# A two-layer hybrid encoder on one core: the rotary chain spread over seven pieces of products, weight splits ranked behind and powers in front, memory's operands made on GpSimd

## The chip, the core and the metric

The kernel runs on one core of one Trainium2 chip. The time is that of one execution on the device in microseconds (us); several runs are made and their median is told. Five engines work side by side, each taking its own instructions strictly in the order in which the program lists them, and each waiting on the others through semaphores: TensorE (PE, matrix products; PEld is its loading of weights), VectorE (DVE), ScalarE (ACT), GpSimd (POOL) and SyncE (SP), which here issues the transfers (DMA).

## The reference

x is 512 tokens by 1024, float32, and passes through two layers. Each layer adds three things to x, each computed from an RMS-normalised copy:

```
x += W_out [ NA-heads(h) || GQA-heads(h) ]        h = RMSNorm(x), one projection w_in
x += MemoryCrossAttention(RMSNorm(x), RMSNorm(mem))   4 heads, 256 memory tokens
x += ConvFFN(RMSNorm(x))                          SwiGLU, width-3 convolution over positions
```

The first has eight heads of neighbourhood attention (NA: each token sees a window of an 8 x 64 grid) and eight query heads on two key-value heads of full attention (GQA). The GQA queries and keys are normalised per head over their 64 channels, multiplied by a gain, and turned by a rotary table:

```
g_q = apply_axial_rope(rms_norm(g_q, q_norm), cos, sin)      # q; k likewise with k_norm
out = stack([x1 * c - x2 * sn, x1 * sn + x2 * c])            # the rotation of a pair of channels
```

The memory's keys and values are `(RMSNorm(mem) * norm_mem_kv) @ w_mem_kv`, for each layer with its own gain.

## The kernel before

**Precision.** Products run in a short float format (fp32r) on split operands: every operand is written as `hi` (a cast) plus `lo` (what the cast lost), and each product is three: hi x hi, hi x lo, lo x hi. So each weight tile that comes from DRAM (`raw`) needs a cast on ACT (`hi`, L255) and a subtraction on POOL (`lo`, L256); this is a *weight split*, made by `emit_split`. Four pairs of hi/lo tiles rotate, so a cast can run only when the products of the weight tile four places earlier are done.

**Layout.** Tokens lie along the free axis (512 columns), channels along the 128 partitions. A projection of 128 output channels is 24 products of 512 columns: 8 slices of input channels by three. The kernel hands them out in *pieces*: generators (`project_qk`, `gqa_project`, `out_na`, ...) that yield after 12 products or so.

**Order.** The attention is a software pipeline (`weave`): at each step the scores of unit s, the normalising of unit s-1, the transposes of unit s-2 and so on are issued, and between them `Filler.run` puts pieces of projections on PE, as many as a budget in nanoseconds allows. PE and SP keep the order in which the Python code issues (`keep_in_program_order`). ACT, DVE and POOL do not: a list scheduler, with a timeline of its own, orders their instructions by a running number, the priority (`tc.cur_priority`, low first), among those which it believes ready. The result is a fixed order per engine; on the chip nothing overtakes.

**Late work.** `Late` holds functions until so many pieces later; `Filler.step` ticks it after each piece. The rotation of one GQA projection, `gqa_rope` (L785), works on a product tile `pm` through it:

- at once: `xs` = gain x pm (L790, ACT), `sq` = pm squared (L791, ACT), `cc` = gain x pm x cosine table (L792, DVE);
- `swap`, one piece later: four transfers swap channel halves of `xs` into `xr` on the SP queue; eight short products with `pairs` sum the squares per head (the *pairs product*, tile `tr`); two small DVE instructions (L801, L804);
- `rotate`, one piece later: on POOL the power -0.5 (L809), its broadcast into `sq` (L810), sine table times `xr` (L811), plus `cc` (L812);
- `norm`, two pieces later: eight short products with the identity turn the broadcast round into a tile `pr` (the *broadcast product*, tile `mm`), DVE multiplies it by `xr` (L819), and ACT and DVE split the result into hi and lo (L616/L620 for k, L634/L636 for q).

There are five such chains in a layer: k, then query pairs 0, 1, 2, 3 (`GQA_ORDER` has v between 1 and 2). PSUM has four accumulators for `mm`, two for `tr` and two for `sc`; a tile keeps its accumulator until the last reader has run.

**Memory.** `memory_prepare` (L488) makes the memory's operands, eight slices of channels by 256 tokens: ACT multiplies by the gain and casts (L502), DVE computes the rest (L503). It runs in the GQA stage by `MEM_STEPS`.

Of the kernel before, what the change touches and what calls it, by code (L numbers as in the profile page):

```python
# [1 line left out]

# [1 line left out]

# [8 lines left out]
AF = mybir.ActivationFunctionType  # L13
ALU = mybir.AluOpType
# [4 lines left out]
P = 128  # L19
# [5 lines left out]
NB = S // P  # L25
KC = D // P
HD = 64
# [21 lines left out]
GQA_FILL = [2300] * 16 + [3000] * 4  # L49
MEM_FILL = [1, 1, 1, 2, 1, 0, 0, 2, 0, 1, 2]  # L50
MEM_STEPS = [1, 0, 1, 1, 1, 1, 1, 1, 1] + [0] * 11
N_RAW, N_W, AHEAD, AHEAD_HELD, N_WARM, N_LATE, N_FIRST = 3, 4, 2, 5, 10, 4, 3


class InOrder:


    def __init__(self, tc, engine):
        self.tc, self.engine = tc, engine

    def __getattr__(self, name):
        op = getattr(self.engine, name)
        return lambda *a, **k: self.tc.keep_in_program_order(op(*a, **k))  # L63
# [12 lines left out]
        return self.tc.keep_in_program_order(self.engine.matmul(out, lhsT, rhs, **k))  # L76


class Switched:

    def __init__(self, tc, engine, ordered):
        self.tc, self.engine, self.ordered = tc, engine, ordered

    def __getattr__(self, name):
        op = getattr(self.engine, name)
        if self.ordered[0]:
            return lambda *a, **k: self.tc.keep_in_program_order(op(*a, **k))
        return op  # L90


class PartsView:
# [83 lines left out]
def encoder_kernel(ctx: ExitStack, tc: tile.TileContext, t: dict, out: bass.AP):  # L177
    nc = tc.nc
    PE, SP = Counted(tc, nc.tensor), InOrder(tc, nc.sync)
    late = Late()  # L180
    ACT_IN_ORDER = InOrder(tc, nc.scalar)
    ordered = [False]
    ACT, DVE, POOL = [Switched(tc, e, ordered) for e in (nc.scalar, nc.vector, nc.gpsimd)]

    cpool = ctx.enter_context(tc.tile_pool(name="cpool", bufs=1))
    xpool = ctx.enter_context(tc.tile_pool(name="xpool", bufs=1))
# [2 lines left out]
    tpool = ctx.enter_context(tc.tile_pool(name="tpool", bufs=10))  # L189
    spool = ctx.enter_context(tc.tile_pool(name="spool", bufs=24))  # L190
    psum = ctx.enter_context(tc.tile_pool(name="psum", bufs=2, space=PSUM))

    uid = [0]

    def nm(s):
        uid[0] += 1
        return f"{s}_{uid[0]}"

    def rtile(shape, dt=F32R):
        return rpool.tile([P, *shape], dt, tag="r", name=nm("r"), padded_shape=[P, *pad(shape)])  # L200
# [24 lines left out]
    f = lambda ap: ap.bitcast(F32)  # L225
# [3 lines left out]
    done = [0]  # L229
# [11 lines left out]
    def emit_split(act=ACT, cuts=2):  # L241
        n = len(ready)
        key, loads, nk, ncol, eng = plan[n]
        raw = raws[n]
        raws[n] = None
        if key[0] in ("up", "down", "memq", "memo"):
            cuts = 1
        if eng[1:] == "r":
            hi, lo = rtile((nk, ncol)), rtile((nk, ncol))
        else:  # L250
            hi = wpool.tile([P, nk, ncol], F32R, tag="hi", name=nm("hi"))
            lo = wpool.tile([P, nk, ncol], F32R, tag="lo", name=nm("lo"))
        for i in range(cuts):
            k = slice(nk * i // cuts, nk * (i + 1) // cuts)
            act.copy(hi[:, k], raw[:, k])  # L255
            (POOL if eng[0] == "P" else DVE).tensor_sub(lo[:, k], raw[:, k], f(hi)[:, k])  # L256
        ready.append((hi, lo))

    def get_w(key, ahead=AHEAD):
# [115 lines left out]
    mhalf = cpool.tile([P, 16], F32, name="mhalf")  # L375
    nc.vector.memset(mhalf, -0.5)

    def rsqrt(src, n, scale):

        v = small(n)  # L380
        DVE.tensor_scalar(v, src, scale, EPS, op0=ALU.mult, op1=ALU.add)
        r = small(n)
        POOL.tensor_tensor(r, v, mhalf[:, :n], op=ALU.pow)  # L383
        return r

    def row_rep(rstd, n, tag, bufs):
# [9 lines left out]
    class Norm:  # L396


        def __init__(self, gcol=None, l=None, cols=slice(0, S)):
            self.gcol, self.l, self.acc, self.last, self.cols, self.n = gcol, l, None, None, cols, cols.stop - cols.start  # L400
            if gcol is not None:
                self.hi, self.lo = [xpool.tile([P, KC, S], F32R, tag="xg", name=nm("xg"), bufs=2) for _ in range(2)]
                self.ops = [(self.hi[:, c, :], self.lo[:, c, :]) for c in range(KC)]
# [85 lines left out]
    def memory_prepare(l, raw=None):  # L489

        mops.clear()
        if raw is None:
            raw = load_mem()
            yield
            yield
        for c in range(KC):
            if c % 2 == 0:
                mg = rtile((2, 2, MEMN))
            g = par[:, l, G_MKV + c : G_MKV + c + 1]
            hi, lo = mg[:, 0, c % 2, :], mg[:, 1, c % 2, :]  # L500
            src = raw[c // 4][:, c % 4, :]
            ACT.activation(hi, src, AF.Copy, scale=g)  # L502
            DVE.scalar_tensor_tensor(lo, src, g, f(hi), op0=ALU.mult, op1=ALU.subtract)  # L503
            mops.append((hi, lo))
            if c % 2 == 1:
                yield
# [42 lines left out]
    for l in range(DEPTH):  # L549
# [63 lines left out]
        def split_k(pm, kt, near):  # L613
            rows = [(slice(64 * j, 64 * j + 64), slice(64 - 64 * j, 128 - 64 * j)) for j in range(2)]
            for k, (r, o) in zip(kt, rows):
                ACT.copy(k[r, 0], pm[r])  # L616
                if near:
                    ACT.copy(k[o, 0], pm[r])
            for k, (r, o) in zip(kt, rows):
                DVE.tensor_sub(k[r, 1], pm[r], f(k[r, 0]))  # L620
                if near:
                    DVE.tensor_sub(k[o, 1], pm[r], f(k[r, 0]))

            def double():
                for k, (r, o) in zip(kt, rows):
                    SP.dma_start(f(k[o]), f(k[r]))

            if not near:
                late(2, double)
# [156 lines left out]
        def gqa_rope(g, pm):  # L786

            gain = qkg[:, l, 0:1] if g != "k" else qkg[:, l, 1:2]
            xs, xr, sq, cc = tmp(), tmp(), tmp(), tmp()
            ACT.activation(xs, pm, AF.Copy, scale=gain)  # L790
            ACT.activation(sq, pm, AF.Square)  # L791
            DVE.scalar_tensor_tensor(cc, pm, gain, gtab[0][:, 0], op0=ALU.mult, op1=ALU.mult)  # L792

            def swap():
                for i in range(4):
                    SP.dma_start(xr[32 * i : 32 * i + 32], xs[32 * (i ^ 1) : 32 * (i ^ 1) + 32])
                pv = ps_t()
                for b in range(NB):
                    PE.matmul(pv[:, 2 * b : 2 * b + 2], sq[:, b * P : (b + 1) * P], pairs, start=True, stop=True)
                v = small(2 * NB)  # L800
                DVE.tensor_tensor(v.rearrange("p (b j) -> p b j", j=2), pv[:, 0 : 2 * NB].rearrange("p (b j) -> p b j", j=2),  # L801
                                  r2[0].unsqueeze(2).to_broadcast([P, NB, 2]), op=ALU.mult)

                DVE.tensor_scalar(v, v, *((1.0 / HD, EPS) if g == "k" else (1.0, EPS * HD)), op0=ALU.mult, op1=ALU.add)  # L804
                late(1, lambda: rotate(v))

            def rotate(v):
                r = small(2 * NB)
                POOL.tensor_tensor(r, v, mhalf[:, : 2 * NB], op=ALU.pow)  # L809
                POOL.tensor_copy(sq.rearrange("p (b d) -> p b d", d=HD), r.unsqueeze(2).to_broadcast([P, 2 * NB, HD]))  # L810
                POOL.tensor_mul(xr, xr, gtab[0][:, 1])  # L811
                POOL.tensor_add(xr, cc, xr)  # L812
                late(2, norm)

            def norm():
                pr = ps_mm()
                for b in range(NB):
                    PE.matmul(pr[:, b * P : (b + 1) * P], sq[:, b * P : (b + 1) * P], ident, start=True, stop=True)
                DVE.tensor_mul(pr, xr, pr)  # L819
                if g == "k":  # L820
                    gk.extend(rtile((2, S)) for _ in range(2))
                    split_k(pr, gk, False)
                else:
                    gq[g] = rtile((2, S))
                    split_q(pr, gq[g])

            late(1, swap)


        ga, gpt = {}, {}  # L830
# [134 lines left out]

        if l > 0:
            load_bias(0)
        ordered[0] = False
        units = [project_v(p) if n == "v" else project_qk(n, p) for n, p in NA_ORDER]
        nns = []  # L970
        attn_fill = Filler(
# [2 lines left out]
            close_rows("outg", 2, PartsView(parts, 4), lambda k: whole[k], lambda: nns.append(Norm(G_MQ, l)) or nns[0],  # L974
                       memory_values(1)))
        attn_fill.step(N_FIRST if l == 0 else N_FIRST + 5)
        ordered[0] = False

        def na_quanta(s):
            if s == 3:  # L980
# [97 lines left out]
        fill.finish()  # L1078


        ordered[0] = False
        ffn = nn
        acts = {}

# [220 lines left out]
```

## Time and profile before

| | us |
|---|---|
| median of 3 runs | 1454.72 (1453.51 to 1455.85) |
| the profiled execution | 1452.22 |
| its span, first to last instruction | 1450.4 |
| PE busy | 1377.7 (95%) |
| PEld busy | 1174.0 (81%) |
| DVE busy | 842.4 (58%) |
| ACT busy | 705.6 (49%) |
| POOL busy | 704.0 (49%) |
| mean granted TensorE clock | 0.978 of full |

How to read the views: *slices* are 40 equal parts of the span, a digit is a busy share in tenths, and PEclk is the TensorE clock that was granted, in tenths. *Waits* name who waited for whom, with the sum in us, the number of times and the longest. *Stretches* give, for a part of the span, busy us of PE, PEld, DVE, ACT and POOL, each with a count of instructions, then the granted clock, the share of the DMA engines and GB/s. *Groups* are instructions of one line and shape: count, busy us, mean ns of one, idle time before them and what ended it. The *timeline* has start, length, engine, line, and in brackets how long the engine idled before and what released it.

In the first layer the first softmax of the neighbourhood attention is at 50 us (L702), the first of the GQA stage at 175 us (L852), the first scores of the memory attention are reduced at 318 us (L1029), and the feed-forward part starts at 385 us (L1114). The five rotations stand between 107 us (the first L792) and 182 us, and in the second layer between 817 and 895 us (the last L819).

### The profile page before, as it was taken

What the parts mean: (1) busy time and instruction counts of PE and PEld (TensorE: products, weight loads), DVE (VectorE), ACT (ScalarE), POOL (GpSimd) and SP (SyncE); (2) the same over time, 40 slices, a digit from 0 to 9 for tenths busy, and PEclk for the clock granted to TensorE, in tenths of its full rate; (3) what the DMA queues carried; (4) which work ended last, traced back from release to release, by engine and by line L of the source; (5) the groups of instructions that cost most, each with busy time, mean ns of one, the idle gap of its engine ahead of it and who ended that gap; (6) DMA issues with size and microseconds to landing.
All of it is one profiled execution on the core that took longest, in us unless ns stands there. A gap on an engine that the chain in (4) does not pass through costs nothing. (4 is left out here: it accounts for less than half of the span.)

```text
span 1450.4 us, 19227 instructions
## 1 busy us (share of the span) xinstructions
PE 1377.7 (95%) x7092; PEld 1174.0 (81%) x7092; DVE 842.4 (58%) x1437; ACT 705.6 (49%) x1308; POOL 704.0 (49%) x509
## 2 busy tenths in 40 slices
PE   7999689999999999999999887999899999999997
PEld 6987579877888888888888766898788888888887
DVE  5664387446488258448446545764637861871874
ACT  5674377656444233333556644776554432431441
POOL 2356546653544444444645555566254444444451
PEclk8998899999999999999999988999999999999999
DMA  7552312321333333332355323124223333323321
GB/s 231 139 149 79 100 30 67 80 87 56 90 99 94 98 99 88 104 102 81 112 155 157 103 70 87 44 74 117 58 59 102 102 101 89 100 86 105 98 77 58
DMA packets 218173, 138.83 MB, mean 96 GB/s; under 512 B 5984, under 2 KB 211040, under 8 KB 218080
## 3 DMA queue, kind: packets, MB, share of 16 engines
q1 hardware_dynamic: 218080, 137.60, 33.2%
q8 instruction: 56, 0.92, 0.3%
q14 instruction: 37, 0.30, 0.1%
HBM read 125.00 MB, written 2.10 MB: 88 GB/s over the span
## 5 line engine op out<-in xcount | busy, mean ns | idle before, releaser
L256 POOL TENSOR_TENSOR lo<-raw,hi 128x1024 fp32r<-128x1024 f32 (+2 forms) x268 | 498.2, 1871 | 542.9 <-ACT hi L255 522.9
L76 PE MATMUL mm<-xg,hi 128*128 128x512 f32 x1984 | 627.5, 398 | 2.3 <-ACT xg L63 2.0
L76 PEld LDWEIGHTS mm<-xg,hi 128*128 128x128 f32 x1984 | 376.4, 192 | 79.2 <-ACT xg L63 2.4
L255 ACT CAST hi<-raw 128x512 fp32r<-128x512 f32 (+2 forms) x276 | 224.1, 836 | 350.6 <-PE mm L76 299.7
L76 PE MATMUL mm<-xg,lo 128*128 128x512 f32 x992 | 391.9, 395 | 0.0
L76 PE MATMUL mm<-r,hi 128*128 128x512 f32 (+1 forms) x1160 | 336.7, 374 | 2.7 <-DVE r L451 2.0
L76 PEld LDWEIGHTS mm<-r,hi 128*128 128x128 f32 x1160 | 211.1, 189 | 41.5 <-DVE r L451 2.8
L1129 DVE SCALAR_TENSOR_TENSOR t<-t,par,t 128x7 f32<-128x7 f32 (+1 forms) x352 | 203.8, 646 | 34.0 <-ACT t L1122 34.0
L76 PEld LDWEIGHTS mm<-xg,lo 128*128 128x128 f32 x992 | 189.9, 191 | 41.1 <-DVE lo L256 0.5
L76 PE MATMUL mm<-r,lo 128*128 128x512 f32 (+1 forms) x580 | 216.1, 373 | 0.0
L76 PEld LDWEIGHTS mm<-r,lo 128*128 128x128 f32 x580 | 109.5, 189 | 19.3
L457 POOL TENSOR_SCALAR t<-t,s 128x512 f32<-128x512 f32 (+1 forms) x112 | 66.0, 603 | 120.5 <-DVE s L852 62.5
L1114 DVE TENSOR_TENSOR t<-mm,rep 128x512 f32<-128x512 f32 x88 | 60.1, 687 | 77.6 <-PE mm L76 62.3
L1131 ACT ACTIVATE t<-t 128x512 f32<-128x512 f32 x44 | 27.9, 633 | 138.8 <-DVE t L1129 138.8
L1135 DVE TENSOR_TENSOR r<-t,r 128x512 fp32r<-128x512 f32 x44 | 90.5, 2056 | 7.3 <-ACT r L1134 4.1
L1158 DVE TENSOR_TENSOR xT<-xT,mm 128x512 f32<-128x512 f32 x32 | 21.9, 685 | 106.8 <-PE mm L76 106.8
L76 PE MATMUL sc<-r,r 128*128 128x256 f32 (+1 forms) x352 | 74.2, 343 | 4.3 <-DVE r L451 1.8
L63 PE MATMUL tr<-ident,t 128*128 128x128 f32 x456 | 63.1, 275 | 14.4 <-DVE r L451 8.5
L63 PEld LDWEIGHTS tr<-ident,t 128*128 128x128 f32 x456 | 52.8, 141 | 23.3 <-issue 12.6
L1122 ACT ACTIVATE t<-t,par 128x512 f32<-128x512 f32 x88 | 66.8, 806 | 2.4 <-DVE t L1114 2.4
L76 PE MATMUL mm<-r,r 128*128 128x256 f32 (+1 forms) x428 | 62.0, 297 | 0.0
L76 PEld LDWEIGHTS sc<-r,r 128*128 128x128 f32 x352 | 52.9, 195 | 11.2 <-ACT r L450 3.0
(133 smaller groups left out, 1534.3 us busy)
## 6 DMA issues: line engine op xcount, KB each, us to landing
raw<-in_w_up SPq DMA_DIRECT2D x88, 512.0 KB, 3.9
raw<-in_w_in SPq DMA_DIRECT2D x34, 512.0 KB, 5.0
raw<-in_w_down SPq DMA_DIRECT2D x32, 448.0 KB, 3.9
raw<-in_w_mem_kv SPq DMA_DIRECT2D x16, 512.0 KB, 3.8
raw<-in_w_down SPq DMA_DIRECT2D x16, 512.0 KB, 4.3
r<-in_bias SPq DMA_DIRECT2D x16, 384.0 KB, 5.7
r<-r SPq DMA_DIRECT2D x22, 256.0 KB, 5.1
raw<-in_w_out SPq DMA_DIRECT2D x8, 512.0 KB, 4.6
```

The source lines that it names most:

```text
L63: return lambda *a, **k: self.tc.keep_in_program_order(op(*a, **k))
L76: return self.tc.keep_in_program_order(self.engine.matmul(out, lhsT, rhs, **k))
L255: act.copy(hi[:, k], raw[:, k])
L256: (POOL if eng[0] == "P" else DVE).tensor_sub(lo[:, k], raw[:, k], f(hi)[:, k])
L457: eng.tensor_scalar(e, e, sums[:, col : col + 1], 1.0, op0=ALU.mult, op1=ALU.mult)
L1114: DVE.tensor_mul(u, us[side], ffn.rep)
L1122: ACT.activation(cc, u, AF.Identity, bias=par[:, l, CB + ch : CB + ch + 1], scale=w[1])
L1129: DVE.scalar_tensor_tensor(cc[:, dst], u[:, src], wi, cc[:, dst], op0=ALU.mult, op1=ALU.add)
L1131: ACT.activation(cs[0], cs[0], AF.Silu)
L1135: DVE.tensor_sub(acts[j][1], cs[0], f(acts[j][0]))
L1158: DVE.tensor_add(xT[m], xT[m], pm)
```

## The change

Five edits. First, the rotation's waits: `swap` comes two pieces after its product tile instead of one, `norm` three pieces after `rotate` instead of two, and what followed the broadcast products (L819 and the split) becomes a function `split` of its own one piece later; from the product tile to the split there are seven pieces instead of four. Second, a context manager `behind(n)` shifts the scheduler's priority for what is issued inside it. Third, weight splits outside the feed-forward part, after the first weight has been taken, are ranked 45 behind. Fourth, the power -0.5 of the norms and the power and broadcast of the rotation are ranked 40 in front. Fifth, `memory_prepare`: POOL multiplies the memory by the gain in place, ACT copies (casts) it, and POOL subtracts, where ACT and DVE did it before. The rest takes away a switch for in-order issue, which was off wherever it stood.

```diff
-N_RAW, N_W, AHEAD, AHEAD_HELD, N_WARM, N_LATE, N_FIRST = 3, 4, 2, 5, 10, 4, 3
+W_BEHIND, N_RAW, N_W, AHEAD, AHEAD_HELD, N_WARM, N_LATE, N_FIRST = 45, 3, 4, 2, 5, 10, 4, 3
...
+    @contextmanager
+    def behind(n):
+        at = tc.cur_priority
+        tc.cur_priority = at + n
+        yield
+        tc.cur_priority = at
...
-        for i in range(cuts):
-            k = slice(nk * i // cuts, nk * (i + 1) // cuts)
-            act.copy(hi[:, k], raw[:, k])
-            (POOL if eng[0] == "P" else DVE).tensor_sub(lo[:, k], raw[:, k], f(hi)[:, k])
+        with behind(W_BEHIND if done[0] and key[0] not in ("up", "down") else 0):
+            for i in range(cuts):
+                k = slice(nk * i // cuts, nk * (i + 1) // cuts)
+                act.copy(hi[:, k], raw[:, k])
+                (POOL if eng[0] == "P" else DVE).tensor_sub(lo[:, k], raw[:, k], f(hi)[:, k])
...
         r = small(n)
-        POOL.tensor_tensor(r, v, mhalf[:, :n], op=ALU.pow)
+        with behind(-40):
+            POOL.tensor_tensor(r, v, mhalf[:, :n], op=ALU.pow)
...
-            ACT.activation(hi, src, AF.Copy, scale=g)
-            DVE.scalar_tensor_tensor(lo, src, g, f(hi), op0=ALU.mult, op1=ALU.subtract)
+            POOL.tensor_scalar(src, src, g, 1.0, op0=ALU.mult, op1=ALU.mult)
+            ACT.copy(hi, src)
+            POOL.tensor_sub(lo, src, f(hi))
...
             def rotate(v):
                 r = small(2 * NB)
-                POOL.tensor_tensor(r, v, mhalf[:, : 2 * NB], op=ALU.pow)
-                POOL.tensor_copy(sq.rearrange("p (b d) -> p b d", d=HD), r.unsqueeze(2).to_broadcast([P, 2 * NB, HD]))
+                with behind(-40):
+                    POOL.tensor_tensor(r, v, mhalf[:, : 2 * NB], op=ALU.pow)
+                    POOL.tensor_copy(sq.rearrange("p (b d) -> p b d", d=HD), r.unsqueeze(2).to_broadcast([P, 2 * NB, HD]))
                 POOL.tensor_mul(xr, xr, gtab[0][:, 1])
                 POOL.tensor_add(xr, cc, xr)
-                late(2, norm)
+                late(3, norm)
...
             def norm():
                 pr = ps_mm()
                 for b in range(NB):
                     PE.matmul(pr[:, b * P : (b + 1) * P], sq[:, b * P : (b + 1) * P], ident, start=True, stop=True)
+                late(1, lambda: split(pr))
+
+            def split(pr):
                 DVE.tensor_mul(pr, xr, pr)
...
-            late(1, swap)
+            late(2, swap)
```

More of the change, by code (lines that the diff above doesn't have):

```diff
@@ L1 @@
-from contextlib import ExitStack
+from contextlib import ExitStack, contextmanager
 import numpy as np
@@ L76, in matmul, with __init__ @@
         return self.tc.keep_in_program_order(self.engine.matmul(out, lhsT, rhs, **k))
-class Switched:
-    def __init__(self, tc, engine, ordered):
-        self.tc, self.engine, self.ordered = tc, engine, ordered
+class Free:
+    def __init__(self, engine):
+        self.engine = engine
     def __getattr__(self, name):
[L87 to L90, printed above, removed]
+        return getattr(self.engine, name)
 class PartsView:
@@ L181, in encoder_kernel @@
     ACT_IN_ORDER = InOrder(tc, nc.scalar)
-    ordered = [False]
-    ACT, DVE, POOL = [Switched(tc, e, ordered) for e in (nc.scalar, nc.vector, nc.gpsimd)]
+    ACT, DVE, POOL = Free(nc.scalar), Free(nc.vector), Free(nc.gpsimd)
     cpool = ctx.enter_context(tc.tile_pool(name="cpool", bufs=1))
@@ L967, in encoder_kernel @@
             load_bias(0)
-        ordered[0] = False
         units = [project_v(p) if n == "v" else project_qk(n, p) for n, p in NA_ORDER]
@@ L976, in encoder_kernel @@
         attn_fill.step(N_FIRST if l == 0 else N_FIRST + 5)
-        ordered[0] = False
         def na_quanta(s):
@@ L1078, in encoder_kernel @@
         fill.finish()
-        ordered[0] = False
         ffn = nn
```

## The prediction

> **What bounds the kernel now.** I read the page's head and slices first, then TensorE's waits, then stretches around them, then the timeline.
>
> ```profile
> span 1450.4 us, 19227 instructions
> PE   7999689999999999999999887999899999999997
> PEclk8998899999999999999999988999999999999999
> ```
>
> TensorE is busy in nine tenths or more of nearly every slice, so what can be won is its idle time and the time at a lower clock. Both stand in the same slices: the fourth to sixth (109 to 218 us) and the 23rd to 25th, which are the two stretches with the rotations.
>
> ```profile
> 100.00:200.00 100.00, 77.01 (x391) 64.25 (x390) 51.14 (x101) 50.09 (x110) 55.71 (x56) 0.90 0.31 85
> 800.00:900.00 100.00, 80.15 (x415) 68.91 (x414) 45.91 (x99) 48.31 (x107) 54.43 (x53) 0.86 0.32 88
> PE tr L76 <- ACT t L791: 13.1, 8, 2.5
> PE mm L76 <- POOL t L810: 12.4, 2, 6.3
> PE tr L63 <- DVE r L451: 8.5, 2, 4.3
> PE tr L76 <- DVE r L451: 5.5, 2, 2.8
> ```
>
> PE idles 23.0 us in the first stretch and 19.9 in the second, 42.9 together, while no other engine but its own weight loading is busy for more than 56%. So these are delays in chains, not a full engine. The four waits, 39.5 us, are the rotation's own steps: pairs products that wait for the square (L791) or for a free accumulator (L451), the broadcast products that wait for L810, the transposes of v and of the attention behind evictions (L451). What comes after each is slow too:
>
> ```profile
> 108.30:116.00 7.70, 7.70 (x27) 6.54 (x28) 0.88 (x3) 0.00 (x0) 5.96 (x5) 0.56 0.31 93
> 126.00:132.00 6.00, 6.00 (x24) 4.92 (x24) 2.48 (x11) 0.12 (x1) 4.70 (x4) 0.72 0.74 197
> 153.20:157.00 3.80, 3.78 (x12) 3.19 (x13) 1.16 (x2) 0.59 (x1) 0.00 (x0) 0.55 0.00 0
> 179.70:184.00 4.30, 4.24 (x14) 3.76 (x15) 1.81 (x3) 1.31 (x3) 0.00 (x1) 0.51 0.01 4
> 818.00:823.40 5.40, 5.35 (x21) 4.50 (x22) 0.93 (x3) 0.04 (x1) 4.49 (x4) 0.68 0.46 131
> 834.00:840.00 6.00, 6.00 (x20) 4.90 (x21) 1.24 (x4) 0.00 (x0) 4.58 (x4) 0.56 0.75 198
> 863.00:877.00 14.00, 11.93 (x37) 9.65 (x38) 2.22 (x5) 2.79 (x5) 6.95 (x6) 0.63 0.31 85
> 894.00:898.00 4.00, 4.00 (x14) 3.29 (x14) 2.77 (x5) 2.31 (x5) 0.00 (x0) 0.59 0.00 0
> ```
>
> Length times (1 - granted clock) is what PE loses: 3.4 + 1.7 + 1.7 + 2.1 = 8.9 us, and 1.7 + 2.6 + 5.2 + 1.6 = 11.1 us. So 42.9 + 20.0 = **62.9 us** is all that the rotations and their neighbours cost; per stall of over 2 us (five a layer: twice L451, twice L791, once L810) the clock's price is 20.0 / 10 = 2.0 us.
>
> Why the steps are late, at one place each:
>
> ```profile
> 124.33 1.05 PE L76 MATMUL tr<-pairs,t 128*128 128x2 f32 x8 [2.54 <-ACT t L791]
> 120.98 1.12 ACT L255 CAST hi<-raw 128x512 fp32r<-128x512 f32 x2
> 122.13 1.07 ACT L450 CAST r<-tr 128x512 fp32r<-128x512 f32 x2
> 123.09 0.70 ACT L790 ACTIVATE t<-mm,qkg 128x512 f32<-128x512 f32 x1
> 123.67 0.61 ACT L791 ACTIVATE t<-mm 128x512 f32<-128x512 f32 x1
> ...
> 174.93 1.65 POOL L809 TENSOR_TENSOR s<-s,mhalf 128x8 f32<-128x8 f32 x1
> 176.56 1.36 POOL L457 TENSOR_SCALAR t<-t,s 128x512 f32<-128x512 f32 x2
> 177.89 1.26 POOL L812 TENSOR_TENSOR t<-t,t 128x512 f32<-128x512 f32 x1
> 179.09 0.61 POOL L810 COPY t<-s 128x512 f32<-128x512 f32 x1
> ```
>
> The square stands on ACT behind a weight split's casts and two evictions; the broadcast stands on POOL behind the power, a softmax's scaling and the cosine sum.
>
> **The change part by part.** The order in which the changed program stands on each engine can be read without running it. PE has the same instructions; only the short rotation products and memory's moved. All four engines keep their old order except from the first rotation to the later GQA stage, in each layer. So everything outside costs the same, and the sum is made in two places. There I followed PE from accumulator to accumulator by the semaphores, with these durations beside the ones above:
>
> ```profile
> L256 POOL TENSOR_TENSOR lo<-raw,hi 128x512 fp32r<-128x512 f32 x122 | 154.9, 1294 | 103.6 <-ACT hi L255 99.1 <-DMA r<-r 4.2
> L457 POOL TENSOR_SCALAR t<-t,s 128x256 f32<-128x256 f32 x48 | 22.5, 485 | 49.2 <-DVE s L702 48.8
> L470 POOL TENSOR_TENSOR r<-t,r 128x256 fp32r<-128x256 f32 x16 | 11.7, 733 | 15.7 <-ACT r L469 15.7
> L503 DVE SCALAR_TENSOR_TENSOR r<-r,par,r 128x256 fp32r<-128x256 f32 x16 | 7.5, 499 | 0.4 <-ACT r L502 0.3
> L620 DVE TENSOR_TENSOR r<-mm,r 64x512 fp32r<-64x512 f32 x20 | 13.8, 689 | 7.4 <-ACT r L616 6.1 <-ACT r L618 1.0
> L616 ACT CAST r<-mm 64x512 fp32r<-64x512 f32 x20 | 11.6, 580 | 2.5 <-DVE mm L607 2.1
> L518 DVE TENSOR_REDUCE t<-r 128x256 f32<-128x1024 f32 x2 | 3.8, 1958 | 0.0
> 475.00:500.00 25.00, 25.00 (x112) 20.67 (x112) 4.91 (x6) 5.26 (x5) 10.71 (x6) 1.00 0.37 105
> 133.37 1.11 PE L76 MATMUL mm<-r,r 128*128 128x256 f32 x8
> 134.32 1.06 PE L76 MATMUL mm<-ident,t 128*128 128x128 f32 x8
> 135.77 0.53 ACT L708 ACTIVATE t<-t,s 128x256 f32<-128x256 f32 x1
> 193.61 0.58 PE L76 MATMUL tr<-ones,t 128*128 128x1 f32 x4 [1.16 <-DVE xg L451]
> 194.81 1.29 PE L63 MATMUL tr<-ident,t 128*128 128x128 f32 x8 [0.62 <-DVE xg L451]
> ```
>
> *The spread itself.* A product of 512 columns takes 25 / 112 = 0.223 us at full clock, a piece of 12 about 2.7; a value block and a set of broadcast products 0.95 and 0.8 to 1. The pairs product of k now follows a piece, and the 2.8 us for a free `tr` go, with their clock. The pairs products of 0 wait some 0.9 us: the casts still stand ahead (1.12 + 1.07 + 0.70 + 0.61 = 3.5 us on ACT, which begins them about 1 us late, against 3.6 us of transposes and products). Those of 1 and 2 wait for nothing. Those of 3 come, as before, only a score block (1.0) after their piece, with casts ahead (1.12 + 0.70 + 0.61 = 2.4): 1.5 us stay. v's transposes have their accumulators free, and 4.3 us go. The swap transfers are a piece later on SP, behind a weight's transfer at times; POOL needs them only with the power done, so they cost nothing unless that transfer waits.
>
> *A new wait.* There are four `mm` accumulators, and the tile of the broadcast products now lives a piece longer. The next owner of k's tile is the first piece of v, and in the new order that piece waits for the second subtraction of k's split (L620). From the last product of pair 1 on, ACT does two casts (1.12), a scaling (0.53), L790 and L791 of pair 1 (0.70 + 0.61) and two halves of k (2 x 0.58), DVE then two subtractions (2 x 0.69): 5.5 us, plus an estimated 0.3 for the exponentials of scores still running; PE has the broadcast (0.8) and the value block (0.95). It idles **4.0 us** a layer. The nearest rows give the bounds: 2.8 (without the casts) to 5.
>
> *The powers in front.* They stand no earlier than their input allows, and the in-order queue still puts other work between power and broadcast. For pair 3 of layer 1, from its pairs product: a split's two subtractions (2.6, of which 2.3 lie behind it), power 1.65, two scalings 1.36, L811 1.28, then four of memory's new multiplications (4 x 0.485 = 1.9) and the broadcast 0.61: 9.1 us, against 6.0 of PE's work (broadcast of 2, 18 products, scores). **3.2 us** of 6.2 stay. In layer 2 the queue holds eight of those multiplications (3.9), L478 (as long as one subtraction, 1.3), two subtractions (2.6), power, four scalings (2.7), L811 and the broadcast: some 12.5 us against 6.5, **6.0 us** stay of 6.3; the broadcast of 2 waits 0.5.
>
> *Memory's operands.* Each layer takes 8 x 0.499 = 4.0 us from DVE and gives POOL 8 x (0.485 + 0.733) = 9.7 us; a copy on ACT costs what the activation did. Besides the above it shows once: in layer 1 DVE makes the memory's squares (2 x 1.96) and then waits for POOL's second four multiplications, with the evictions of a transpose behind it: about 4 us at the statistics (`ones`) and the transposes behind them, where 1.16 + 0.62 stood. If POOL's slack (45% idle) were gone, all 9.7 would be PE's.
>
> Sum: idle that stays, layer 1: 0.9 + 4.0 + 1.5 + 3.2 + 4.0 + 0.5 of old small waits = 14.1; layer 2: 0.9 + 4.0 + 1.5 + 0.5 + 6.0 + 0.4 = 13.3; about 2 us of this is the last products' drain, which the old waits do not count either: 25.4. Stalls of over 2 us: three and two, x 2.0 = 10.0. Won: 62.9 - 25.4 - 10.0 = 27.5, so 1452.2 - 27.5 = 1424.7 for a profiled execution; the median of the runs before is 2.5 above theirs, hence **1427 us**.
>
> On the clock the Trainium skill, "TensorE: Matmul & The Clock Gate", "HAM oscillation — how this bites in real kernels", allows idle gaps up to about 3.4 us. The rows differ: the stalls of 2.54 us and 2.8 us are followed by a granted 0.72 and 0.56. By the page only three of my five stalls would cost clock, 4 us less, 1423.
>
> **The rivals.** *The waits that I left go too* (the accumulator or POOL's queue has more room than my additions): of 42.9 + 20.0 stay the small ones, 8 us: 1452.2 - 54.9 + 2.5 = 1400. For it: ACT and POOL are half idle. Against it: both waits stand in the order itself.
>
> *The new waits eat the gain*: each hop that I took at zero adds up, stalls are half longer (38) and ten pass 2 us (20): won 5, 1450. For it: four accumulators and ACT's unchanged casts ahead of the square; ranking splits behind has moved none of those at the pairs products of 0 and 3. Against: six of the ten pairs products then wait for nothing, and k's is the only late tile that a piece of weights follows at once.
>
> *Slower: memory on POOL.* If all 9.7 us of each layer delay the scalings that the transposes need, idle is 19.4 + 20 (accumulator and last broadcast, twice 10) + 8, and ten stalls cost 20: 67.4 against 62.9, 1459. It decides once more than about 7.5 us a layer land on PE. Against it: POOL idles 44 of the first stretch's 100 us, and a unit's scalings (1.36) are due a whole step before its transposes.
>
> **How the numbers follow.** Chances: forecast 0.70, waits gone 0.12, gain eaten 0.12, slower 0.06. Range 1408 to 1444: the forecast with the new accumulator wait at 2.8 to 5, stalls' clock price between 1.6 and 3.4 (the rows of 894 and 108 us), POOL's ends, and parts of its neighbours. 0.2% (2.9 us) is what a measurement can tell: faster takes the first two and two thirds of the third (0.90), same 0.03, slower 0.07.
>
> **What would show it.** Right: the waits on L791 fall from 13.1 to about 5, both on L451 nearly vanish, a new wait of an `mm` product on DVE's L620 of some 8 us in two appears, the wait on the broadcast stays at 9 to 10 us, the granted clock of both stretches rises to about 0.95; outside, nothing moves. Wrong: GQA-stage transposes that wait for POOL scalings, or an idle PE before v's first piece of far more than 4 us.

## The result and the profile after

The changed kernel takes 1416.79 us (median of 4 runs, 1414.88 to 1420.02) where the kernel before took 1454.12 beside it: a ratio of 0.9751, 95% interval 0.972 to 0.9783. The profiled execution took 1417.6 us, 34.6 less than the 1452.2 of before.

The head and the slices of the changed kernel's page:

```profile
span 1415.8 us, 19240 instructions
PE 1364.5 (96%) x7092; PEld 1165.1 (82%) x7092; DVE 838.2 (59%) x1421; ACT 703.2 (50%) x1308; POOL 724.0 (51%) x541
PEclk8999999999999999999999999999999999999998
```

TensorE is idle for 1415.8 - 1364.5 = 51.3 us; before it was 1450.4 - 1377.7 = 72.7. So 21.4 us are idle time that went, and 13.2 are the same 7092 products at a higher clock. In the clock's row the 8s of the two rotation stretches, four slices before, have become 9s.

Five of TensorE's waits in the changed kernel (waited for, us in total, times, longest), and the two stretches (us, then busy time of PE, PEld, DVE, ACT and POOL, PE's clock, DMA share, GB/s). In the new file L798 is the square (L791 before), L818 the broadcast's copy (L810), L627 the split's subtraction (L620), L457 the subtraction of an eviction (L451), and L532 belongs to memory's statistics:

```profile
PE mm L76 <- POOL t L818: 7.4, 3, 3.9
PE mm L76 <- DVE r L627: 7.1, 2, 3.5
PE tr L76 <- ACT t L798: 5.5, 4, 2.3
PE tr L63 <- DVE s L532: 1.8, 1, 1.8
PE tr L63 <- DVE xg L457: 1.8, 2, 1.2
```

```profile
100.00:200.00 100.00, 89.68 (x504) 76.89 (x504) 65.27 (x122) 62.84 (x142) 74.06 (x82) 0.97 0.34 90
800.00:900.00 100.00, 86.39 (x472) 73.48 (x472) 58.93 (x116) 58.84 (x135) 71.83 (x80) 0.95 0.25 70
```

Idle time in the stretches is 10.3 and 13.6 us, 23.9 in place of 42.9; at a clock of 0.97 and 0.95 another 3 + 5 = 8 us are lost. The prediction's 20.0 for the clock before was summed over eight short rows; the two whole rows of before (0.90 and 0.86) give 10 + 14 = 24, idle time included. The square's wait fell from 13.1 to 5.5 and the broadcast's from 12.4 to 7.4; both waits of a `tr` product on the subtraction (8.5 and 5.5) are gone; a new one, of an `mm` product on L627, stands in each layer.

The place of the new wait, in the timeline of all engines:

```profile
123.52 1.05 PE L76 MATMUL mm<-ident,t 128*128 128x128 f32 x8
123.84 1.15 ACT L260 CAST hi<-raw 128x512 fp32r<-128x512 f32 x2
124.33 1.20 PE L76 MATMUL mm<-r,r 128*128 128x256 f32 x8
124.68 0.70 DVE L830 TENSOR_TENSOR mm<-t,mm 128x512 f32<-128x512 f32 x1 [0.51 <-PE mm L76]
124.87 0.53 ACT L715 ACTIVATE t<-t,s 128x256 f32<-128x256 f32 x1
125.28 0.69 ACT L797 ACTIVATE t<-mm,qkg 128x512 f32<-128x512 f32 x1
125.85 0.61 ACT L798 ACTIVATE t<-mm 128x512 f32<-128x512 f32 x1
126.33 1.17 ACT L623 CAST r<-mm 64x512 fp32r<-64x512 f32 x2
127.53 1.39 DVE L627 TENSOR_TENSOR r<-mm,r 64x512 fp32r<-64x512 f32 x2 [2.15 <-ACT r L623]
129.07 0.47 PE L76 MATMUL mm<-xg,hi 128*128 128x512 f32 x1 [3.54 <-DVE r L627]
```

k's broadcast products end at 124.3. Their multiplication follows at once, the casts of k's split stand behind four other groups of ACT's, and v's first piece may start after the two subtractions behind them. Between broadcast and v's piece TensorE has one value block (1.2 us).

### The profile page after: what moved, and what is told of

It reads as the page before. It is cut to its first block, busy times and chain, and to the rows that moved or that the text cites. A ratio compares the mean times of both kernels' runs of the same rounds, so it can differ in the third digit from the quotient of the medians.

```text
span 1415.8 us, 19240 instructions
## 1 busy us (share of the span) xinstructions
PE 1364.5 (96%) x7092; PEld 1165.1 (82%) x7092; DVE 838.2 (59%) x1421; ACT 703.2 (50%) x1308; POOL 724.0 (51%) x541
## 5 line engine op out<-in xcount | busy, mean ns | idle before, releaser
L76 PE MATMUL mm<-xg,hi 128*128 128x512 f32 x1984 | 620.1, 394 | 9.0 <-DVE r L627 7.1
L76 PEld LDWEIGHTS mm<-xg,hi 128*128 128x128 f32 x1984 | 371.2, 189 | 85.1 <-issue 7.4
```

## The experiments

The change has four parts that alter the program: a first shift (`late(2, swap)`: pairs products and swap transfers a piece later), a second (`late(3, norm)`: broadcast products a piece later behind the power), a third (`late(1, split)`: the split a piece behind the broadcast), and memory's operands on GpSimd. The ranks do nothing: with `behind` set to 0 everywhere the built program has the same instructions in the same order on all five engines. Each shift also moves what stands behind it in the chain: `late(2, swap)` puts the power, the broadcast and the split a piece back too.

Ratios are to the kernel before in runs beside each kernel; its median was 1449 to 1454 us from group to group, so ratios are what is compared.

| kernel | 1st shift | 2nd | 3rd | memory on | median us | ratio (95%) |
|---|---|---|---|---|---|---|
| changed kernel | yes | yes | yes | POOL | 1416.8 | 0.9751 (0.972 to 0.9783) |
| e1_spread_alone | yes | yes | yes | ACT, DVE | 1418.4 | 0.9763 (0.9748 to 0.9777) |
| e2_memory_alone | no | no | no | POOL | 1451.2 | 0.9992 (0.998 to 1.0003) |
| e3_split_at_once | yes | yes | no | POOL | 1426.6 | 0.9817 (0.9803 to 0.9832) |
| e6_swap_only | yes | no | no | POOL | 1415.0 | 0.9744 (0.9725 to 0.9762) |
| e7_norm_only | no | yes | no | POOL | 1462.3 | 1.0068 (1.0046 to 1.0089) |
| e8_before_swap | yes | no | no | ACT, DVE | 1411.7 | 0.9737 (0.9719 to 0.9754) |
| e9_swap_split | yes | no | yes | POOL | 1411.0 | 0.9731 (0.9711 to 0.9751) |

### Memory's operands: e1 and e2

e1 is the changed kernel with the old lines of `memory_prepare`; e2 is the kernel before with the new ones (its diff is shown, e1 takes the same lines back):

```diff
-            ACT.activation(hi, src, AF.Copy, scale=g)
-            DVE.scalar_tensor_tensor(lo, src, g, f(hi), op0=ALU.mult, op1=ALU.subtract)
+            POOL.tensor_scalar(src, src, g, 1.0, op0=ALU.mult, op1=ALU.mult)
+            ACT.copy(hi, src)
+            POOL.tensor_sub(lo, src, f(hi))
```

> The changed kernel with memory's operands made on ACT and DVE again, as before; only the rotation's spread is left. Theory (memory's multiplications stand in POOL's queue ahead of the last broadcasts): the wait of an mm product on the broadcast (L818 in the changed kernel, 7.4 us in three) falls to under 2 us, the wait on DVE's s ahead of memory's transposes (1.8 us) goes too, with some 2 us of clock: 7 to 11 us less than the changed kernel's 1416.8, 1406 to 1410. Rival (POOL is half idle, and the multiplications only move the waiting about): within 3 us of the changed kernel, 1414 to 1420. A second rival (DVE's relief of 4 us a layer is what brought part of the gain): 1420 or more.

> The kernel before with memory's operands made on GpSimd, and nothing else changed. Theory: the wait on the broadcast, 12.4 us in two before, grows by the four to eight multiplications in front of it (1.9 us in layer 1, up to 3.9 in layer 2), and memory's statistics by 2 to 4 us: 5 to 11 us slower than before, 1459 to 1465. Rival (hidden in POOL's idle time): within 3 us of before, 1451 to 1457. Rival (DVE's relief pays): under 1451.

The times are 0.9763 beside 0.9751, and 0.9992: the move is worth nothing that shows, alone or with the spread. TensorE's waits of e1 (its L797, L817 and L856 are the changed kernel's L798, L818 and L857):

```profile
PE sc L76 <- ACT t L856: 4.3, 1, 4.3
PE tr L63 <- DVE xg L457: 3.2, 2, 2.8
PE mm L76 <- POOL t L817: 2.2, 2, 1.8
```

The theory of e1 was right on the wait and wrong on the time: without memory's multiplications in POOL's queue the wait on the broadcast falls from 7.4 to 2.2 us. But the time does not, since the products behind then wait for other things, a softmax's scores for ACT (4.3) and transposes for DVE (3.2, where the changed kernel has 1.8). In e2 the broadcast's wait grew by only 1.3:

```profile
PE mm L76 <- POOL t L818: 13.7, 2, 7.5
```

So the first rival's time held for both, for e2 narrowly (1451.2 in 1451 to 1457): the waiting only moves.

### The split a piece later: e3

```diff
-                late(1, lambda: split(pr))
+                split(pr)
```

> The changed kernel with the rotation's split issued right behind the broadcast products, not a piece later; TensorE's order stays the same. Theory (the new wait of v's first piece comes from k's accumulator, which is held a piece longer): the wait of an mm product on DVE's L627 (7.1 us in two) goes, with the 3 us that the clock costs after it: 1405 to 1409. Rival (the split's multiplication, now early in DVE's order, waits there for TensorE and holds up evictions behind it): those waits return elsewhere, among them products that wait for tr or for the softmax, and the time stays within 4 us of the changed kernel, 1413 to 1421.

It is slower, 0.9817, 0.0066 or 9.6 us above the changed kernel, also above the rival's range, and the wait that I wanted to take away is unchanged:

```profile
PE tr L76 <- DVE t L526: 9.8, 1, 9.8
PE mm L76 <- DVE r L627: 7.1, 2, 3.5
```

The theory falls: v's first piece does not wait because k's accumulator is held a piece longer by the third shift. In both kernels k's multiplication runs straight behind the broadcast. What the third shift is worth shows elsewhere: in layer 1 memory's statistics product (`ones`) waits 9.8 us for DVE's last addition of memory's squares (L526), which with the split at once stands behind the split of rotation 3 (its subtractions end at 173.6 us and the addition begins at 178.1; in the changed kernel the addition begins at 169.3 and the subtractions at 173.4). So the rival had the kind of wait right, a wait for DVE elsewhere, but not its size.

### What a stall costs: e4

```diff
+            if g == "v":
+                for _ in range(2):
+                    fillp = ps_s()
+                    for _ in range(12):
+                        tc.keep_in_program_order(nc.tensor.matmul(fillp[:, 0:P], ident, ident, start=True, stop=True))
             pm = ps_mm()
```

> The changed kernel with 24 needless products of 128 columns (0.13 us each, 3.2 us) into score accumulators right ahead of v's first piece, so that TensorE works through nearly all of the 3.54 us in which it waited. The same wait, but no stall: what changes is the clock behind it. Theory (a stall of this length costs 1 to 2 us of clock): the stretch of 4 us behind it, at a granted 0.61 in layer 1 of the changed kernel, comes to over 0.9, and the time falls by 2 to 4 us, to 1413 to 1415. Rival (the clock there is not this stall's doing): the stretch stays at 0.6 to 0.7 and the time is the same or up to 2 us more, 1416 to 1419.

The 24 products stand as 48 in the trace and took 5.27 us, not 3.2, longer than the wait. TensorE's timeline, of the changed kernel behind the rows shown above (value block at 124.33, v's piece at 129.07) and then of e4:

```profile
133.48 0.95 PE L76 MATMUL tr<-pairs,t 128*128 128x2 f32 x8
```

```profile
124.10 1.20 PE L76 MATMUL mm<-r,r 128*128 128x256 f32 x8
125.14 5.52 PE L773 MATMUL sc<-ident 128*128 128x128 f32 x48
130.41 0.71 PE L76 MATMUL mm<-xg,hi 128*128 128x512 f32 x2
133.25 0.95 PE L76 MATMUL tr<-pairs,t 128*128 128x2 f32 x8
```

From the value block to the end of v's first piece it is 133.48 - 124.33 = 9.15 us with the stall and 133.25 - 124.10 = 9.15 with 5.27 us of needless work in its place. Stretches of 4 us behind the stall, and behind the needless work:

```profile
129.07:133.07 4.00, 4.00 (x11) 3.19 (x12) 0.63 (x1) 0.00 (x0) 1.03 (x1) 0.61 0.00 0
```

```profile
130.41:134.41 4.00, 4.00 (x26) 3.50 (x25) 0.17 (x1) 0.00 (x0) 0.00 (x0) 1.00 0.00 0
```

The clock behind is 1.00 in place of 0.61. So the low clock is the stall's doing, and the stall of 3.54 us costs 9.15 less the 1.04 of the value block and the 2.84 of the piece at full clock, 5.3 us in all, 1.7 of it by the clock (the value block and the piece are the steps from 124.10 to 125.14 and from 130.41 to 133.25 in e4). The whole time is 1416.0 us (0.9747): the fill used up what the clock gave back. The theory held for the clock and not for the time, because the fill was longer than planned.

### Where the broadcast stands: e5

```diff
-                late(3, norm)
+                late(4, norm)
```

> The changed kernel with the broadcast products called four pieces behind the power in place of three (late(4, norm)); the split still follows a piece later. k's broadcast then comes behind v's first piece, which takes an accumulator that has long been free, and the last broadcast gives POOL a piece (2.7 us) more. Theory (the wait of v's first piece comes from where k's broadcast stands: right ahead of it, so that its split is still to come): the wait on L627 (7.1 us in two, and 3.0 of clock behind it) goes, the wait on L818 (7.4 in three) falls to 2 or less: 12 to 16 us less than the changed kernel's 1416.8, 1401 to 1405. Rival (four accumulators are too few wherever the broadcast stands: the products behind it wait for the split of k in place of v's): the wait on L627 stays at 5 us or more, 1410 to 1416. Rival (the later split of the last rotation meets memory's statistics, as when it was split at once): a wait of the ones products of 5 us or more, 1415 to 1425.

1422.2 us, ratio 0.9792 (0.9774 to 0.981): by the middle values slower than the changed kernel, though the two intervals overlap (0.9774 to 0.9783). My reading of the order was wrong: four pieces behind the power, k's broadcast goes past the value block and still stands ahead of v's first piece, now right ahead of it.

```profile
PE mm L76 <- DVE t L799: 7.6, 2, 4.2
PE mm L76 <- POOL t L818: 6.5, 1, 6.5
```

v's first piece waits as long as before, but for another accumulator, that of pair 1, which the cosine product (L799) reads last. The broadcast's wait goes from layer 1 and is 6.5 in layer 2. No expectation held as written: the wait on L627 went, as the theory said, but the accumulators are still too few, as the first rival said, and the time is above that rival's range. It lies in the second rival's range, whose wait of 5 us at the `ones` product did not come (2.8).

### One shift alone: e6, e7, e8

e6 has `late(2, swap)`, `late(2, norm)` and the split at once; e7 `late(1, swap)`, `late(3, norm)` and the split at once; both with memory on POOL. e8 is the kernel before with one number changed:

```diff
-            late(1, swap)
+            late(2, swap)
```

> The changed kernel with one of the three shifts alone: the pairs products and swap transfers a piece later (late(2, swap)); the broadcast two pieces behind the power and the split at once, as before. Theory (the first shift frees the tr accumulators for v's transposes and lets the squares finish): the waits on L457 ahead of tr products (8.5 and 5.5 before) go, those on L798 fall from 13.1 to about 5.5, the wait on the broadcast stays at 12 or so: 13 + 8.5 us of idle and 6 to 10 of clock, 25 to 30 less than before's 1453.2, but for the statistics, which split at once costs up to 10: 1424 to 1438. Rival (the shift only moves the chain back against the products behind it): the waits move to L818 and the time stays at 1440 or more.

> The changed kernel with another of the three shifts alone: the broadcast products three pieces behind the power (late(3, norm)); pairs products as early as before, the split at once. Theory: the wait on L818 (12.4 us in two before) falls to under 3, with 3 to 4 us of clock; the waits ahead of the pairs products (L798 13.1, L457 5.5) and v's transposes (L457 8.5) stay; 8 to 14 us less than before, 1439 to 1445. Rival (it is the broadcast's place that held up all the rest): 1425 to 1435. Rival (the chain's end moves into the products behind it): 1450 or more.

> The kernel before with one number changed: late(2, swap) in place of late(1, swap). Theory (the later pairs products are the whole gain; the other two shifts and memory's move pay for one another): 1412 to 1420, within 4 us of the changed kernel. Rival (memory's move to GpSimd is needed with it, because the second shift alone was measured only with it): 1424 or more.

The first shift alone gives 0.9744 and, without memory on POOL, 0.9737: all of the change's gain. The second alone makes the kernel slower, 1.0068. e6 came out below my range of 1424 to 1438, e8 0.3 us below the lower edge of its range, and e7 in the range of its second rival (1450 or more). TensorE's waits of e6, e7 and e8 in turn (in e8 L791, L810 and L852 are the square, the broadcast's copy and the softmax's reciprocal):

```profile
PE mm L76 <- POOL t L818: 10.2, 4, 6.7
PE tr L76 <- DVE t L526: 8.5, 1, 8.5
PE tr L76 <- ACT t L798: 5.4, 6, 1.4
```

```profile
PE tr L76 <- ACT t L798: 18.6, 8, 3.4
PE tr L63 <- DVE r L457: 10.8, 2, 5.4
PE tr L76 <- DVE s L863: 10.5, 1, 10.5
```

```profile
PE tr L76 <- DVE s L852: 9.0, 1, 9.0
PE tr L76 <- ACT t L791: 4.8, 5, 1.4
PE mm L76 <- POOL t L810: 4.7, 4, 2.2
```

In e6 the square's wait is down to 5.4, the waits for a free `tr` accumulator are gone, and there is no wait on L627 at all. In e6's timeline k's broadcast, the split's subtractions and v's first piece are these:

```profile
118.75 1.14 PE L76 MATMUL mm<-ident,t 128*128 128x128 f32 x8
122.30 1.40 DVE L627 TENSOR_TENSOR r<-mm,r 64x512 fp32r<-64x512 f32 x2
124.38 0.63 PE L76 MATMUL mm<-xg,hi 128*128 128x512 f32 x2
```

The broadcast begins 5.6 us ahead of v's piece, with scores, a piece of pair 1 and the value block between, and the subtractions end at 123.7, before v needs the accumulator. In e7 the early pairs products wait as before or longer, and the later broadcast of rotation 3 meets memory's statistics (10.5 us). I had expected 8 to 14 us less, since the broadcast's wait of 12.4 would go; that wait did go, but those on squares, transposes and statistics grew.

e6 and e7 are the cleanest pair. From the product tile to the broadcast there are five pieces in both (2 + 1 + 2 and 1 + 1 + 3), and k's broadcast stands at the same place in TensorE's order. What stands a piece later in e6 is `swap` (pairs products, transfers) and the POOL steps of `rotate`, and the ratio is 0.9744 against 1.0068. So the gain does not come from a later broadcast but from the steps ahead of it. These were not moved apart from each other; the waits that went are those of the pairs products and of the `tr` accumulators.

In all three kernels memory's `ones` product waits for DVE, 8.5, 10.5 and 9.0 us; where memory's operands are made makes little difference to this.

### Putting parts together: e9 to e12

e9 is the changed kernel with `late(2, norm)`. e10 has the second and third shift for rotation 3 alone. e11 is e6 with memory's statistics a step later, e12 the kernel before with the first and third shift and that step:

```diff
-MEM_STEPS = [1, 0, 1, 1, 1, 1, 1, 1, 1] + [0] * 11
+MEM_STEPS = [1, 0, 1, 0, 1, 1, 1, 1, 1, 1] + [0] * 10
```

> The changed kernel without its second shift: pairs products a piece later, the split a piece later, the broadcast two pieces behind the power as before. Theory (the later split is worth what it takes from ACT's and DVE's queues at the last rotation, where memory's squares stand behind it): the wait of the ones product on L526, 8.5 us with the first shift alone, falls under 3, and no wait of v's first piece comes, since k's broadcast stands further ahead: 1407 to 1411. Rival (the accumulator that is held a piece longer costs a wait of its own, L627 or L799 of 3 us or more in each layer): 1413 to 1419.

> The changed kernel with the second and third shift for rotation 3 alone; k, 0, 1 and 2 have only the pairs products later. Theory (the second and third shift help where the last broadcast waits for POOL, and cost where k's broadcast meets v's first piece): no wait on L627, the last broadcast in layer 2 waits 3 to 4 us in place of 6.7, memory's ones product some 2 to 3 in place of 8.5: 1404 to 1410. Rival (the last rotation's later split meets memory's statistics in any order): a wait at the ones product of 6 us or more, 1412 to 1418.

> The changed kernel with the first shift alone (as in the run of that name) and memory's statistics product, with all of memory's steps behind it, one step of the attention later (a 0 put into MEM_STEPS after the squares). Theory (the 8.5 us of the ones product on L526 is a product that stands too early in TensorE's order, not a chain that is too long): the wait falls under 1 us and 7 to 10 us go: 1405 to 1408. Rival (the wait is DVE's and only moves to the softmax products behind, which DVE also serves): 1412 to 1416.

> The kernel before with three changes that each was a little faster than the first shift with memory on GpSimd (ratio 0.9744): memory's operands left on ACT and DVE (0.9737), the split a piece later (0.9731), memory's statistics a step later (0.9734). Theory (each takes away a wait of its own place, so the gains add): 0.9744 less 0.0007, 0.0013 and 0.0010 is 0.9714, some 1.7 us less than the best of them. Rival (all three relieve the one stretch behind the last rotation of layer 1, where one wait takes the place of another, so they don't add): 0.973 to 0.976.

They came to 1411.0 us (0.9731), 1414.1 (0.9753, 0.9736 to 0.977), 1411.3 (0.9734, 0.9717 to 0.9752) and 1413.5 (0.9742, 0.9722 to 0.9762; six runs that spread from 1406.3 to 1416.1). All of these intervals overlap with e6's. The waits of e9 and of e11:

```profile
PE tr L76 <- DVE xg L457: 3.4, 1, 3.4
```

```profile
PE tr L63 <- DVE xg L457: 5.2, 2, 5.1
```

In e9 no wait on L627 came, and the `ones` product waits 3.4 us in place of 8.5. In e11 that product waits for nothing, and a transpose near it waits 5.1 for an eviction of DVE's. e10's `ones` product waits 2.9. Each edit thus takes away most of its wait at the last rotation of layer 1, and the ratio moves by -0.0013, +0.0009 and -0.0010 from e6, none of it clear of the intervals. That the next products wait for DVE in turn is shown by e11's row; for e10 it is not shown. e9's time met its theory; e10's time is in its rival's range, though without that rival's wait; e11's lies between theory and rival. The gains don't add: e12's rival held, and the theory's 0.9714 is just below the interval. No kernel here is surely faster than e8, the one number; by the middle values e8, e9 and e11 lie 1.4 to 2 thousandths below the changed kernel, within the intervals.

## Why the prediction was right, and where not

**The bound and the place.** Right. Of the 21.4 us of idle time won, 19.0 are in the two rotation stretches (42.9 became 23.9) and 2.4 outside. Of the clock the prediction counted 20.0 us lost before, in short rows; whole rows give 24 before and 8 after. All that the clock gave in the whole kernel is 13.2 us, so most of it is here, but the rows do not divide it exactly.

**The spread itself.** Right in each place: the pairs product of k waits for nothing, that of 0 for 0.71 us (0.9 predicted), those of 3 for 1.79 and 2.29 (1.5), and v's transposes for nothing. What the prediction did not do was ask which of the three shifts brings this. It is the first: one number gives 0.9737. The other two are a loss and its repair: with the first shift in, the second costs 0.0073 when the split is at once (e3 against e6), and the third then gives 0.0066 back (changed kernel against e3). Without the second the third is worth 0.0013, within the intervals.

**The new wait.** Its place, releaser and size were right: 3.54 us in each layer where I had 4.0, on the second subtraction of k's split, and the ACT work ahead of it as listed. Its cause was half wrong. I said that the tile of the broadcast products lives a piece longer. e3 takes the extra piece away and the wait stays at 3.54 us; e6 takes the second shift away as well and the wait is gone; e9, which takes only the second away, has none either, and nor has e7 with the second alone. It takes the first and the second together: six pieces behind its product tile, k's broadcast stands right ahead of the value block and v's piece, so that TensorE has 1.2 us of work where the chain to the last subtraction takes 4.7 (124.33 to 129.07).

**The powers in front, and the last broadcast.** I had 3.2 us in layer 1, 0.5 and 6.0 in layer 2; they were 2.29, 1.17 and 3.88. The prediction said that ranking the splits moves nothing at the pairs products; in fact no rank moves anything, the powers' included. Memory's multiplications did stand ahead of the broadcast (e1: 2.2 us without them), so the mechanism was right. In layer 1 POOL's queue was oversized: 8.2 us from the end of pair 3's pairs product to the end of the copy in place of 9.1. In layer 2 it is the other side, TensorE's, that was undersized:

```profile
847.08 1.05 PE L76 MATMUL tr<-pairs,t 128*128 128x2 f32 x8 [2.29 <-ACT t L798]
849.30 1.36 PE L76 MATMUL mm<-ident,t 128*128 128x128 f32 x8 [1.17 <-POOL t L818]
860.28 0.62 POOL L818 COPY t<-s 128x512 f32<-128x512 f32 x1
860.96 2.08 PE L76 MATMUL mm<-ident,t 128*128 128x128 f32 x8 [3.88 <-POOL t L818]
```

From the end of the pairs product (848.1) to the end of the copy (860.9) it is 12.8 us beside my 12.5. But TensorE spent 9.0 of them where I had 6.5: 1.2 waiting for the broadcast of 2, and 7.8 at work, 1.6 of it because the clock was 0.60 from 849.30 to 853.30. My 12.5 came near by luck: the terms that I listed for it add up to 14.0, and four of the eight multiplications had run before the pairs product ended.

**Memory's operands.** The term of 4 us at the statistics of layer 1 measured 1.83. I counted the move as a cost of this and of the broadcast's growth. e1 and e2 say that it costs nothing (with it the ratio is 0.0012 and 0.0008 lower; between e8 and e6 0.0007 higher): what it takes at the broadcast is waited for elsewhere without it, at ACT and DVE (e1's rows). Here a cost was counted that is not there.

**The clock.** 10.0 us predicted, 8 by the whole rows of the stretches. I had three stalls of over 2 us in layer 1 and two in layer 2; there are two (3.54 and 2.29) and three (3.54, 2.29 and 3.88), so that the number of five is partly luck. The 4 us behind each lose 1.2 to 1.7 us in place of 2.0. The limit of 2 us is not sharp: 2.20 us (e6), 2.23 (e8) and one of the ten that the prediction priced, 2.07 (160.26 us in the kernel before), are followed by a clock of 1.00, and 2.03 in e9 by 0.53. The changed kernel's stretches behind the stalls of 1.79 us and 2.29 us:

```profile
157.70:161.70 4.00, 3.97 (x26) 3.60 (x27) 2.84 (x5) 2.02 (x6) 3.89 (x4) 1.00 0.40 94
167.08:171.08 4.00, 4.00 (x19) 3.86 (x20) 4.00 (x6) 1.08 (x3) 4.00 (x7) 0.57 0.00 0
```

The Trainium skill, "TensorE: Matmul & The Clock Gate", section "HAM oscillation — how this bites in real kernels", allows idle gaps up to about 3.4 us. The measurement differs: 2.29 us of waiting is followed by a clock of 0.57, and 3.54 us by 0.61, which e4 shows to be the wait's doing. By the Trainium skill the stall of 2.29 us would have cost no clock; this row does not bear that out. The prediction's count of three stalls above that figure has its 4 us at the statistics split over two waits.

**The sum.** For a profiled execution I had 1424.7 and it was 1417.6. Of the 7.1 us, 3.9 are idle time (21.4 won where 17.5 were predicted): 1.5 in the stretches, where layer 1 kept 10.3 for the 14.1 of the terms, layer 2 13.6 for 13.3 (errors that cancel: the last broadcast 2.1 less, but 0.8 more at the pairs products of 3, 0.7 at the broadcast of 2, and 1.8 at transposes that wait for L457, where I had 0.4 of small waits), and the 2 us of drain that I took off do not show, and 2.4 outside. 3.2 are the clock (13.2 of busy time won against 10.0). The rest of the 10 us to the median is the 2.3 that I added from the profiled execution to the median (2.5, rounded), and the 0.8 by which the changed kernel's median lies below its profiled execution. Of the rivals, no wait at all (1400) was too good: the accumulator and the broadcast did wait. The gain eaten and the slower kernel need waits that the whole spread does not bring; the second shift alone does bring them (e7, 1.0068).

## What to carry to other kernels

When a chain of small steps is spread over a pipeline, measure each shift alone before adding up their benefits: here one step moved by one piece was the gain, and the next was a loss that a third repaired. The wait for k's accumulator was set here by how much other work lies between the products that fill it and the next owner, so look at what stands between the two in TensorE's order before asking how long the tile lives. Where several engines stand half idle and one product waits, moving an operation off a queue may only hand the wait to the next queue, as with memory's operands here; try it alone first.

## What the runs showed of the hardware that was not expected

One addition on DVE, the same 128x256 with both operands in SBUF, takes between 0.42 us and 3.40. Timelines of the kernel before, where POOL was idle until 192.38, and of e7:

```profile
191.79 0.42 DVE L519 TENSOR_TENSOR t<-t 128x256 f32<-128x256 f32 x1
192.38 0.69 POOL L457 TENSOR_SCALAR t<-t,s 128x512 f32<-128x512 f32 x1 [12.68 <-DVE s L852]
```

```profile
196.72 2.51 POOL L261 TENSOR_TENSOR lo<-raw,hi 128x512 fp32r<-128x512 f32 x2
198.83 3.40 DVE L526 TENSOR_TENSOR t<-t 128x256 f32<-128x256 f32 x1
199.18 2.78 POOL L510 TENSOR_TENSOR r<-r,r 128x256 fp32r<-128x256 f32 x4
```

In e7 the addition starts while POOL is in a subtraction, and ends at 202.23, 0.27 us behind the last of four further POOL subtractions (201.96). The Trainium skill, "SBUF — State Buffer", section "🔬 SBUF: two separate sides", says that an operation of DVE with two SBUF inputs and one of GpSimd exclude each other for a whole instruction. The rows agree, and show DVE behind five POOL instructions in a row, not one. The other kernels fit: the addition takes 0.41 or 0.42 us where POOL was idle at its start (the kernel before, e1, e8), and in e2, e3, e6 and the changed kernel 1.35, 1.71, 2.50 and 1.08 us, each time with its end 0.28 to 0.30 us behind the last of POOL's instructions on two tensors. Beside POOL's multiplications of one tensor it takes 0.65 (e4). So 3.0 of e7's 10.5 us at the `ones` product lie in this addition (3.40 in place of 0.42). That the two exclude each other is argued from these times; no run changes this alone, and in e8 the product waits 9.0 us with the addition at 0.41.

In e4, 5.27 us of needless products in the place of a stall of 3.54 cost nothing from one end to the other: there the low clock in the microseconds behind cost 1.7 us more, about half as much as the wait itself.
